# A hybrid decoder layer: the first branch's gates moved behind the attention and formed by products by sevens, the attention in single banks, sums in DRAM in 4 KB rows

## The chip, the cores and the metric

One core of one Trainium2 chip runs one decoder layer in float32. The metric is the device time of one launch in microseconds, median of three runs. Five queues of instructions work side by side on the core: PE (matmul, with its weight loads), DVE (VectorE), ACT (ScalarE), POOL (GpSimd) and SP (SyncE, here only DMA issues). Each works off its own instructions in order and waits at semaphores for the others.

## The reference

256 positions of 2048 channels go through three parallel token mixers and a feed-forward block. `h` is the normalised input, `p = h @ w_in` is cut into the mixers' inputs:

- A: `glu -> causal depthwise conv (31) -> LayerNorm -> silu -> @ w_a_out`
- B: `gelu(uv); u * (tril(W_s) LN(v) + b) -> @ w_b_out`
- C: attention with 16 query heads of 64 in 4 groups, and three sets of keys and values (compressed, selected, window) whose results are weighted by sigmoid gates per head, `-> @ w_c_out`

```python
g_a, g_b, g_c = jnp.split(jax.nn.sigmoid(merge_g), 3, axis=-1)
mixed = (g_a * y_a + g_b * y_b + g_c * y_c) @ w_o[l]
x = x + rms_norm(mixed, norm_mix_post[l])
...
u = causal_depthwise_conv(h @ w_up[l], ffn_conv_w[l], ffn_conv_b[l])
x = x + rms_norm((jax.nn.silu(u_g) * u_v) @ w_down[l], norm_ffn_post[l])
```

With 256 positions all four blocks of keys that a query may select are taken, so selected and window attention are both plain causal attention.

## The kernel before, in words

**Products.** A float32 weight piece of 128 x 1024 is loaded by SP into `wraw` (5 buffers), ACT copies it into a rounded part `whi`, DVE subtracts and leaves `wlo` (4 buffers each). A product of an activation tile with 512 columns is three matmuls, hi x hi, hi x lo, lo x hi (`mm_t`, L246 to L249). The positions are two tiles of 128, called t = 0, 1.

**Products by sevens.** Two tiles of the contraction (a pair), two halves of positions and two halves of columns are eight products of 128 x 128 by 512. Class `Seven` (L1034) forms them from seven products, Strassen's way in Winograd's form. The sums of activations are made on the core (`sums4`, L942, in `sh`), the sums of weights by POOL in DRAM before they are needed (`ahead_steps`, L132): a step copies a block of a weight into an `ahead` tile or adds one to it. The steps are one list, issued a few at a time by `ahead_by` (L155): a tiny `tick` copy waits for a mark of progress, then so many steps follow. `pooled` keeps them in order. A step that adds waits for the landing of the step whose result it adds to. `in_sevens` (L1114) interleaves plain tiles with sevens; `combine` adds up the four side banks, the totals (L1257) add them to the main banks.

**PSUM.** Eight banks of 128 x 512 float32: four of the pool `PS` (tag `acc`) and four of a second pool, which during the attention is cut into two single banks and one double (`banks(2, 1)`).

**Stages on PE, in the trace's time.** v of branch B (to 50 us), input of A, then u of B, keys, values and queries (to 296), then `branch(0)`: four times gates and outputs of B; `branch(1)`: the same of A (to 619), then gates and outputs of C (619 to 748), `w_o` (to 836), the feed-forward's up products (to 1328), down products (to the end). The gates of A and B are plain products of 16 tiles each, those of C take sevens for 4 of 8 pairs.

**Beside the products.** Convolution, norms and the attention are generators in a queue `bg`, of which `pump` takes steps between pieces of the main stream. The attention (`attn`, L961) has eight units, of a tile of positions, a half of the groups, and a branch. A unit's scores `s` are matmuls on 64 of the 128 rows, alternately lower and upper half (`in_turns`); its probabilities are transposed (`pp`), and the value products `O` fill 64 of 128 columns, again in pairs of halves. The compressed part enters `O` as one product with the tile `vbd`, which POOL fills (L969) from `pct`.

**The order.** The kernel's framework sets the order on each queue from dependencies, priorities and a timeline that it reckons; `issue_after` and `in_line` bind single instructions to others.

Of the kernel before, what the change touches and what calls it, by code (L numbers as in the profile page):

```python
# [30 lines left out]
D = 2048  # L31
# [17 lines left out]
BA, BB, BC, BG = 2100, 2200, 2200, 6500  # L49
# [15 lines left out]
def block(ctx: ExitStack, tc: tile.TileContext, x, xf, x0, fp, cst, rows, sgw, w1, w2, wf_a, wt_bv, wf_bu, wf_c,  # L65
# [66 lines left out]
    def ahead_steps():  # L132

        quads = [(("g", cp, j), wt_gq[cp, j], 3) for cp in range(2) for j in range(len(GP))]
# [4 lines left out]
        for i, (key, src, sums) in enumerate(quads):  # L139
# [180 lines left out]
    begin = P1.tile([128, T + KT], F32, name="begin")  # L320
# [16 lines left out]
    wz = P1.tile([128, 128], mybir.dt.bfloat16, tag="q", bufs=12, name="wz")  # L337
# [222 lines left out]
    def lna_gen():  # L560
# [61 lines left out]
    bg.append(mark("A"))  # L622
# [75 lines left out]
    def cmp_gen(kv):  # L698
# [22 lines left out]
        th = P1.tile([128, 2, 64], F32, tag="hth", name=f"hth{kv}")  # L721
# [132 lines left out]
    class Unit:  # L854
# [8 lines left out]
        def scores(self):  # L863
# [4 lines left out]
            ep = [Ct_box["ep"][:, r] if br else s8([128, 2, 4, 256], F32, f"ep{self.nm}{r}") for r in range(2)]  # L868
            e = self.e = [t[:, 0] for t in ep]
            self.pt = [t[:, 1].rearrange("p a b -> p (a b)").rearrange("p (k c) -> p k c", k=2) for t in ep]  # L870
            m = self.m = P1.tile([128, 2, 8], F32, tag="am", bufs=2, name="am" + self.nm)
            for b in range(4 // hpb):
                ps = two_banks([128, 2, hpb, nk], f"s{self.nm}{b}")
                in_turns([(ps[:, r, jj], qf[half[r], gg * 4 + b * hpb + jj, qt * 128:qt * 128 + 128],
                           kk[half[r], gg, br, 0:nk], True, True) for jj in range(hpb) for r in (1, 0)])
                for jj in range(hpb):
                    j = b * hpb + jj
                    for r in range(2):
                        V.tensor_tensor_reduce(e[r][:, j, 0:nk], ps[:, r, jj], mk, 1.0, -3e38, ALU.add, ALU.max,
                                               m[:, r, j:j + 1])  # L880
                        yield nk * 1.05 + 130
# [19 lines left out]
        def values(self, O):  # L901
            qt, gg, br = self.at
            e, pt = self.e, self.pt
            for kb in range(qt + 1):
                pp = two_banks([128, 2, 4, 128], f"pp{self.nm}{kb}")
                for r in range(2):
                    for j in range(4):
                        PE.transpose(pp[:, r, j], e[r][:, j, kb * 128:kb * 128 + 128], ident)
                for r in range(2):
                    with ExitStack() as order:  # L910
                        if r:
                            order.enter_context(tc.issue_after(a))
                        a = S.activation(pt[r][:, kb], pp[:, r].rearrange("p j t -> p (j t)"), AF.Copy).ins
                yield 200
            if br == 0:
                PE.matmul(O.rearrange("p j t -> p (j t)"), lhsT=vbd[:, gg], rhs=spread.rearrange("p j t -> p (j t)"),
                          start=True, stop=False, skip_group_check=True)
            in_turns([(O[half[r]].rearrange("p j t -> p (j t)"),
                       vsw[:, kb, br * 256 + (2 * gg + r) * 64:br * 256 + (2 * gg + r) * 64 + 64], pt[r][:, kb],
# [4 lines left out]
            Ct = Ct_box["t"]  # L924
# [6 lines left out]
    sh = P1.tile([128, 3, 2, 4, 128], R, name="sh")  # L931
    sh2 = []

    def sh_of(j):

        if j >= 3 and not sh2:
            sh2.append(s8([128, 2, 2, 4, 128], R, "sh2"))
        return sh[:, j] if j < 3 else sh2[0][:, j - 3]
# [3 lines left out]
    def sums4(a0, a1, dst, nm):  # L942
# [6 lines left out]
        for i, x in enumerate((p, q)):  # L949
            d = [dst[:, j, 2 * i:2 * i + 2].rearrange("p a b -> p (a b)") for j in range(2)]  # L950
# [3 lines left out]
    def input_sums(j):  # L954
# [3 lines left out]
        sums4(a[0], a[1], sh_of(j), f"h{j}")  # L958
        yield 0

    def attn():  # L961

        units = [Unit(qt, gg, br) for qt in range(2) for gg in range(2) for br in range(2)]
        yield from units[0].scores()
        for n, u in enumerate(units):
            if n + 1 < len(units):
                yield from units[n + 1].scores()
# [4 lines left out]
            if n % 2 and n // 2 < 3:  # L972
                yield from input_sums(n // 2)
# [4 lines left out]
    for qt in range(2):  # L978
        bg.append(apart(cmp_attn(qt)))

    def alloc_C():
        Ct_box["t"] = s16(P1, [128, 8, 2, T], R, "Ct")
        Ct_box["ep"] = s16(P1, [128, 2, 2, 4, T], F32, "ep")
        banks(2, 1)
        yield 0

    def single():
        banks(4, 0)
        yield 0
    bg.append(alloc_C())  # L990
# [43 lines left out]
    class Seven:  # L1034
# [25 lines left out]
        def seven(self, quad, key, a, tt, acts, nm, last):  # L1060
# [7 lines left out]
            if sums > 2:  # L1068
                nc.sync.dma_start(r[:, 512:], src[:, 2])
                parity[0] ^= 1  # L1070
                tt = tt[:, (L, U)[parity[0]]]
            if sums > 3:
                nc.sync.dma_start(tt, src[:, 3])
            (hb, lb), (ha, la), (ht, lt), (hr, lr) = (ring(nm + x) for x in "batr")
            high(hb, b)
            if sums > 2:
                rest(lb, b, hb)
                high(ha, a)
                if sums == 3:
                    fixed(V, V.tensor_add, tt, b[:, U], r[:, U])  # L1080
# [18 lines left out]
            for bank_, act, h, l, c in ((self.c[0][1], s4, hb, lb, L), (self.c[0][0], h1, hb, lb, U),  # L1099
# [14 lines left out]
    def in_sevens(pr, plain, pairs, REST, between, act, acts, keys, spare, tt, nm):  # L1114
# [3 lines left out]
        rest_ = REST[2:]  # L1118
# [806 lines left out]
```

## Time and profile before

| | |
|---|---|
| median of 3 runs | 1556.17 us (1554.79 to 1556.34) |
| span of the profiled execution, first to last instruction | 1554.3 us |
| median less this span | 1.9 us |
| PE matmuls | 8125 records |
| PE, DVE, ACT, POOL busy | 1547.5, 1289.7, 953.6, 214.2 us |
| queue of SP's loads (q1), of POOL's steps (q0) | 325.27 MB, 81.93 MB |

The page gives no other time of the profiled execution than its span. Busy times of PE overlap from one matmul to the next, so a busy share of 100% says that PE had no gap, and the distance between two starts says what a matmul costs. A row of the timeline is start, duration, engine, line, operation, output <- inputs, shape, count. A matmul that takes two passes over plain float32 (`s`, `O`) leaves two records. In the windows view each row is a stretch, its length, and the busy time of PE, PEld, DVE, ACT and POOL with the number of instructions, then PE's granted clock, the DMA share and GB/s.

### The profile page before, as it was taken

How to read it: one execution, taken by the hardware profiler on the slowest of the kernel's cores; microseconds unless marked ns; L12 is line 12 of the kernel's file. 1: busy time of each engine (PE TensorE's matmuls, PEld its weight loads, DVE VectorE, ACT ScalarE, POOL GpSimd, SP SyncE). 2: the span in 40 equal slices, each digit the busy share in tenths (PEclk: the TensorE clock that was granted, in tenths of full speed). 3: DMA queues.
4: the chain of work that ended last, by engine and by line, in shares of the span. 5: the costliest groups of instructions: out<-in, count | busy, mean ns of one | idle time of the engine just before them, and what ended most of it. 6: DMA issues, size and time to landing. Idle time of an engine off the chain costs nothing.

```text
span 1554.3 us, 23223 instructions
## 1 busy us (share of the span) xinstructions
PE 1547.5 (100%) x8125; PEld 1318.1 (85%) x8125; DVE 1289.7 (83%) x2189; ACT 953.6 (61%) x1518; POOL 214.2 (14%) x319
## 2 busy tenths in 40 slices
PE   9999999999999999999999999999999999999998
PEld 8888889888877777888888888888888888888887
DVE  7899999878675554878887888888888888899898
ACT  7644554467486756556565665656565656677774
POOL 1011350200111111000000022221212121100000
PEclk9999999999999999999999999999999999999999
DMA  9697996977777898767784699999999999989995
GB/s 369 197 269 234 274 295 211 286 255 242 212 223 234 218 258 259 237 221 253 269 263 157 208 294 307 303 281 262 270 271 264 266 256 268 317 279 348 318 374 210
DMA packets 130069, 409.33 MB, mean 263 GB/s; under 512 B 14240, under 2 KB 16016, under 8 KB 129184
## 3 DMA queue, kind: packets, MB, share of 16 engines
q1 hardware_dynamic: 97344, 325.27, 61.0%
q0 software_dynamic: 32032, 81.93, 23.3%
q8 instruction: 63, 1.03, 0.3%
q10 hardware_dynamic: 576, 0.66, 0.1%
q14 instruction: 54, 0.44, 0.1%
HBM read 399.67 MB, written 77.86 MB: 307 GB/s over the span
## 4 chain that ended last, share of the span: by engine, by line
PE 97%; DVE 1%; ACT 1%; issue 0%; DMA 0%; DVEq 0%; ACTq 0%
PE ps L226 29%; PE ps L233 15%; PE pd1a L1049 4%; PE pd0b L1049 4%; PE pg L248 3%; PE pg L249 3%; PE pg L247 3%; PE pd0a L1049 3%; PE pd1b L1049 3%; PE py L249 3%; PE py L247 3%; PE py L248 3%; PE pg0a L1049 2%; PE poa L1049 2%; PE pg1a L1049 2%; PE po L248 1%
## 5 line engine op out<-in xcount | busy, mean ns | idle before, releaser
L198 DVE TENSOR_TENSOR wlo<-wraw,whi 128x1024 fp32r<-128x1024 f32 (+1 forms) x376 | 455.4, 1216 | 122.8 <-ACT whi L197 103.2
L197 ACT ACTIVATE whi<-wraw 128x1024 fp32r<-128x1024 f32 (+1 forms) x376 | 394.7, 1055 | 241.6 <-PE ps L226 120.2
L226 PE MATMUL ps<-h2T,whi 128*128 128x512 f32 x1360 | 317.2, 390 | 0.0
L226 PEld LDWEIGHTS ps<-h2T,whi 128*128 128x128 f32 x1360 | 252.5, 188 | 50.3
L233 PEld LDWEIGHTS ps<-h2T,wlo 128*128 128x128 f32 x1360 | 169.4, 192 | 3.6
L233 PE MATMUL ps<-h2T,wlo 128*128 128x256 f32 x1360 | 170.8, 283 | 0.0
L226 PE MATMUL ps<-hT,whi 128*128 128x512 f32 x640 | 152.0, 391 | 0.0
L226 PEld LDWEIGHTS ps<-hT,whi 128*128 128x128 f32 x640 | 118.0, 188 | 22.9
L554 DVE SCALAR_TENSOR_TENSOR cv<-hb,fps,cv 128x256 f32<-128x256 f32 x240 | 103.8, 470 | 0.1
L248 PE MATMUL pg<-wlo,hT 128*128 128x512 f32 x256 | 101.2, 395 | 0.2 <-DVE wlo L198 0.2
L249 PE MATMUL pg<-whi,hT 128*128 128x512 f32 x256 | 101.1, 395 | 0.0
L247 PE MATMUL pg<-whi,hT 128*128 128x512 f32 x256 | 98.9, 394 | 0.3 <-ACT mg L1162 0.3
L1005 DVE TENSOR_TENSOR wlowraw<-wraw,whiwraw 128x1024 fp32r<-128x1024 f32 x58 | 70.4, 1222 | 32.0 <-ACT whiwraw L1005 30.6
L1536 ACT ACTIVATE fa<-fs,fps 128x256 f32<-128x256 f32 x88 | 52.7, 598 | 53.5 <-DVE fs L272 51.5
L233 PEld LDWEIGHTS ps<-hT,wlo 128*128 128x128 f32 x640 | 81.2, 192 | 2.5
L127 POOL DMA_DIRECT2D ahead<-in_wt_dq_dram x91 | 72.1, 906 | 80.1 <-DMA ahead<-in_wt_dq_dram 71.7
L233 PE MATMUL ps<-hT,wlo 128*128 128x256 f32 x640 | 82.8, 284 | 0.0
L1005 ACT ACTIVATE whiwraw<-wraw 128x1024 fp32r<-128x1024 f32 x58 | 61.0, 1058 | 32.4 <-PE py L249 12.7
L269 ACT ACTIVATE t<-ps 128x256 f32<-128x256 f32 x125 | 47.5, 381 | 51.2 <-PE ps L233 28.2
L127 POOL COPY tick<-gh 128x1 f32<-128x1 f32 x44 | 35.2, 800 | 271.6 <-ACT gh L1544 264.0
L248 PEld LDWEIGHTS pg<-wlo,hT 128*128 128x128 f32 x256 | 48.1, 188 | 11.7 <-issue 1.5
L247 PEld LDWEIGHTS pg<-whi,hT 128*128 128x128 f32 x256 | 47.9, 188 | 11.0 <-issue 0.9
(2173 smaller groups left out, 3085.2 us busy)
## 6 DMA issues: line engine op xcount, KB each, us to landing
wraw<-in_wf_up_dram SPq DMA_DIRECT2D x176, 512.0 KB, 6.1
ahead<-in_wt_dq_dram POOLq DMA_DIRECT2D x74, 512.0 KB, 9.3
wraw<-in_wt_g_dram SPq DMA_DIRECT2D x64, 512.0 KB, 5.0
wraw<-in_wt_p_dram SPq DMA_DIRECT2D x48, 512.0 KB, 5.7
wraw<-in_wt_dq_dram SPq DMA_DIRECT2D x33, 512.0 KB, 5.5
wraw<-in_wf_a_dram SPq DMA_DIRECT2D x32, 512.0 KB, 4.9
fin<-ahead SPq DMA_DIRECT2D x32, 512.0 KB, 5.7
ahead<-ahead POOLq DMA_DIRECT2D x45, 256.0 KB, 7.1
```

What stands on the lines that cost most here:

```text
L127: in_pool[:] = [op(*args, **kw).ins]
L197: S.activation(hi[:, :n], raw[:, :n], AF.Copy)
L198: V.tensor_sub(lo[:, :n], raw[:, :n], hi[:, :n].bitcast(F32))
L226: ins = PE.matmul(ps, lhsT=ws[k // 8][0][:, c:c + 128], rhs=mov[:, k], start=bool(k == 0 and first), stop=bool(k == n - 1 and not first), ...
L233: ins = PE.matmul(ps[:, 1], lhsT=ws[k // 8][1][:, c:c + 128], rhs=mov[:, k, 0], start=bool(k == 0 and not first), stop=bool(k == n - 1 and ...
L247: PE.matmul(ps, lhsT=xh, rhs=hi, start=first, stop=False)
L248: PE.matmul(ps, lhsT=xh, rhs=lo, start=False, stop=False)
L249: return PE.matmul(ps, lhsT=xl, rhs=hi, start=False, stop=last).ins
L554: V.scalar_tensor_tensor(ca[:, j], hb[:, j, k:k + T], w(j, k), ca[:, j], op0=ALU.mult, op1=ALU.add)
L1005: seq[eng] = [op(*args, **kw).ins]
L1049: ins = PE.matmul(bank, lhsT=a[x], rhs=w[y], start=first and j == 0, stop=bool(last and j == 2), skip_group_check=more).ins
L1536: S.activation(a, s, AF.Identity, bias=fps[:, C_FB + f:C_FB + f + 1], scale=w[2])
```

## The change

- **Order of the branches.** `branch` forms gates and outputs of B only. Then `outs_a` forms A's outputs alone, ungated, into `ya` (DVE copies). The gates of A become columns of the gate products behind it.
- **Gates.** `gates_7` runs four times by sevens, twice for A (i = 0, 1), twice for C (i = 2, 3), for 4 of 8 pairs each. Main and side banks swap between the two pools from one to the next. A's gates are applied by `gate_a`: multiply `ya`, add to `mac`. With `lead` some plain tiles go first, and `then` puts the previous group's totals and `gate_a` behind them.
- **Attention.** It starts with the last part of A's norm (`lnz_gen`), the scores of the first unit and the compressed scores taken in turn, and works off the units of the second tile of positions first. It has to be finished in the first group of gates (`attended`). Scores and transposes take single banks, one per half, from a pool of four throughout. `pump` is scaled by 0.85 from the attention on.
- **Sums.** The weights' four blocks are laid out in another order in DRAM, so that a step that adds two blocks reads them as one row of 4 KB, where it read two rows of 2 KB. There are 32 steps more (eight more pairs), and `ahead_by` takes (4, 8, 8, 8) of them in `branch` and (8, 8, 8, 8) in `outs_a`, where the two branches took (0, 0, 6, 8) and (8, 8, 8, 0).

Three places show how instructions move. On PE, scores and value products of a unit of the second tile of positions; `py`, `pg` are full products, `whi`, `wlo` weights, the number behind a name is its buffer. Before:

```order
L850 MATMUL O_4589<-ep_4435,kkv 64x512
L850 MATMUL O_4589<-ep_4434,kkv 64x512
L850 MATMUL s_4607<-kkv,qf 128x256 x4
L249 MATMUL py_5354<-whi_5394,At 128x512
...
L247 MATMUL pg_5446<-whi_5449,hT 128x512
L850 MATMUL s_4616<-kkv,qf 128x256 x4
L248 MATMUL pg_5446<-wlo_5450,hT 128x512
```

And in the change, of such a unit too:

```order
L853 MATMUL O_4415<-pt_3282,kkv 64x512 x2
L853 MATMUL s_4633<-kkv,qf 128x256
L249 MATMUL py_5234<-whi_5244,At 128x512
L250 MATMUL py_5234<-wlo_5245,At 128x512
L251 MATMUL py_5234<-whi_5244,At 128x512
L249 MATMUL py_5235<-whi_5244,At 128x512
L853 MATMUL s_4632<-kkv,qf 128x256
L853 MATMUL s_4633<-kkv,qf 128x256
L853 MATMUL s_4632<-kkv,qf 128x256
L250 MATMUL py_5235<-wlo_5245,At 128x512
L853 MATMUL O_4415<-ep_4334,kkv 64x512 x2
L853 MATMUL s_4643<-kkv,qf 128x256
```

A group of four scores stood in one piece; now the first of the four stands alone, and its partner on the other half of the array comes four products later, from another bank. On POOL, the fill of `vbd` for the last compressed unit. Before:

```order
L127 DMA ahead_82<-ahead_82 128x512 [waits DMASW2_49,DMASW1_49]
L127 DMA ahead_83<-in_wt_dq_dram 256x512 [waits DMASW3_49]
L969 TENSOR_TENSOR vbd<-pct_4313,cs 128x512 [waits PE_49]
L127 COPY tick<-mac 128x1 [waits DVE_49,Pool_49]
L127 DMA ahead_84<-in_wt_dq_dram 128x1024 [waits DMASW6_49]
```

In the change, with the second and third of the `ya` batches ahead of it:

```order
L129 DMA ahead_90<-in_wt_dq_dram 128x1024 [waits DMASW0_49]
L129 DMA ahead_91<-in_wt_dq_dram 128x1024
L129 COPY tick<-ya 128x1 [waits DVE_49,Pool_49]
L129 DMA ahead_90<-ahead_90 128x512 [waits DMASW2_49,DMASW1_49]
L129 DMA ahead_91<-in_wt_dq_dram 128x1024 [waits DMASW3_49]
L129 DMA ahead_92<-in_wt_dq_dram 128x1024 [waits DMASW6_49]
L129 DMA ahead_92<-in_wt_dq_dram 128x512 [waits DMASW7_49]
L990 TENSOR_TENSOR vbd<-pct_4529,cs 128x512 [waits PE_49]
```

It stood behind the second of the batches that follow `mac` and now stands in the middle of the third that follows `ya`, with DMA steps on both sides. The diff, cut:

```diff
 def pump(ns):
+    if "attn" in marks:
+        ns *= RUSH
...
-        quads = [(("g", cp, j), wt_gq[cp, j], 3) for cp in range(2) for j in range(len(GP))]
+        quads = [(("g", cp, j), wt_gq[cp, j], 3) for cp in range(4) for j in range(len(GP))]
...
             if sums > 2:
-                yield dst[:, 2:], src[:, 0:sums - 2], {}
+                yield dst[:, 2:], src[:, 4 - sums:2], {}
             yield from late
-            yield dst[:, 0:2], src[:, 0:4:2], add
-            late = [(dst[:, b], dst[:, b - 1], add) for b in range(2, sums)]
+            yield dst[:, 0:2], src[:, 1:3], add
+            late = [(dst[:, x], dst[:, y], add) for x, y in ((sums - 1, 1), (2, 3))[:sums - 2]]
...
-                ps = two_banks([128, 2, hpb, nk], f"s{self.nm}{b}")
-                in_turns([(ps[:, r, jj], qf[half[r], gg * 4 + b * hpb + jj, qt * 128:qt * 128 + 128],
+                ps = [bank([128, hpb, nk], f"s{self.nm}{b}{r}") for r in range(2)]
+                in_turns([(ps[r][:, jj], qf[half[r], gg * 4 + b * hpb + jj, qt * 128:qt * 128 + 128],
...
-            for kb in range(qt + 1):
-                pp = two_banks([128, 2, 4, 128], f"pp{self.nm}{kb}")
+            for kb in range(qt, -1, -1):
+                pp = [bank([128, 4, 128], f"pp{self.nm}{kb}{r}") for r in range(2)]
...
-        units = [Unit(qt, gg, br) for qt in range(2) for gg in range(2) for br in range(2)]
-        yield from units[0].scores()
+        units = [Unit(qt, gg, br) for qt in (1, 0) for gg in range(2) for br in range(2)]
+        yield from in_turn(lnz_gen(), apart(cmp_attn(1)), apart(units[0].scores()))
+        marks.add("A")
...
-            ahead_by(mac[:, 0, cb * 512:cb * 512 + 1], ((0, 0, 6, 8), (8, 8, 8, 0))[bi][cb])
+            ahead_by(mac[:, 0, cb * 512:cb * 512 + 1], (4, 8, 8, 8)[cb])
             pump(BUDGET)
+
+    def outs_a():
+        for cb in range(4):
+            py = [PS.tile([128, 512], F32, tag="acc", name=f"py1{cb}{t}") for t in range(2)]
+            for q in range(2):
+                hs = granule(wt_p[(4 + cb) * 2 + q])
+                if cb == 0 and q == 0:
+                    until("A")
...
+                        pe_last[0] = mm_t(py[t], At[:, k, 0, ts], At[:, k, 1, ts], hi[:, c], lo[:, c], k == 0, k == 7)
...
+                    V.tensor_copy(ya[:, t, cb * 512:cb * 512 + 512], py[t])
+            ahead_by(ya[:, 0, cb * 512:cb * 512 + 1], (8, 8, 8, 8)[cb])
...
-    branch(0, lambda: Bt_box["t"])
-    branch(1, lambda: At)
-    until("A")
-    until("C")
+    branch()
+    ya = s16(P1, [128, 2, D], F32, "ya")
+    outs_a()
...
+    def gate_a(cp, gates):
         for n in range(2):
             for t in range(2):
+                cc = slice(cp * 1024 + n * 512, cp * 1024 + n * 512 + 512)
+                V.scalar_tensor_tensor(gates[:, t, n], gates[:, t, n], 1.0, ya[:, t, cc], op0=ALU.add, op1=ALU.mult)
+                V.tensor_add(mac[:, t, cc], mac[:, t, cc], gates[:, t, n])
...
+    prs.append(gates_7(0, (0, 0, 0, 0), 6, attended))
+    prs.append(gates_7(1, (1, 0, 0, 0), 4, gated_a(0)))
+    for cp in range(2):
+        pr = gates_7(2 + cp, (1, 1, 1, 0) if cp else (1, 0, 0, 0), 2 if cp else 4, None if cp else gated_a(1))
```

More of the change, by code (lines that the diff above doesn't have):

```diff
@@ L589, in lna_gen, with lnz_gen @@
         r = rsqrt(P1, var, T, "a")
+        norm["r"] = r
         yield 3400
-        while "gates" not in marks:
-            yield 2400
+    def lnz_gen():
+        r = norm["r"]
         for j in range(8):
@@ L621, in block @@
     bg.append(lna_gen())
-    bg.append(mark("A"))
     BUDGET = BB
@@ L929, in values @@
             yield 650
[L931 to L938, printed above, removed]
+    pt1 = P1.tile([128, 2, 4, 128], F32, name="pt1")
+    sh = P1.tile([128, 4, 2, 3, 128], R, name="sh")
     H1, H2 = slice(0, 128), slice(128, T)
@@ L948, in sums4 @@
         V.tensor_sub(q[:, H2], a0[:, H1], a0[:, H2])
-        for i, x in enumerate((p, q)):
-            d = [dst[:, j, 2 * i:2 * i + 2].rearrange("p a b -> p (a b)") for j in range(2)]
+        first, last = dst
+        for d, x in (([first[:, j, 0:2].rearrange("p a b -> p (a b)") for j in range(2)], p),
+                     ([first[:, j, 2] for j in range(2)], q[:, H1]), (last, q[:, H2])):
             S.activation(d[0], x, AF.Copy)
@@ L957, in input_sums, with g_acts, in_turn @@
             V.tensor_add(a[i], hT[:, 2 * j + i, 0].bitcast(F32), hT[:, 2 * j + i, 1].bitcast(F32))
[L958 to L959 removed]
+        s3.append(P1.tile([128, 2, 128], R, tag="q", bufs=11, name=f"s3{j}"))
+        sums4(a[0], a[1], (sh[:, j], [s3[j][:, i] for i in range(2)]), f"h{j}")
+        yield 3000
+    s3 = []
+    def g_acts(j):
+        return acts_of(j, GP[j], hx, (s3[j][:, 0], s3[j][:, 1]))
+    def in_turn(*works):
+        works = list(works)
+        while works:
+            for w in list(works):
+                try:
+                    yield next(w)
+                except StopIteration:
+                    works.remove(w)
     def attn():
[L963 to L964 removed]
+        units = [Unit(qt, gg, br) for qt in (1, 0) for gg in range(2) for br in range(2)]
+        yield from in_turn(lnz_gen(), apart(cmp_attn(1)), apart(units[0].scores()))
+        marks.add("A")
+        Ct_box["t"] = s16(P1, [128, 8, 2, T], R, "Ct")
         for n, u in enumerate(units):
             if n + 1 < len(units):
[L967 removed]
+                if n == 1:
+                    yield from in_turn(apart(cmp_attn(0)), units[n + 1].scores())
+                else:
+                    yield from units[n + 1].scores()
             if u.at[2] == 0:
@@ L971, in attn @@
             yield from u.weights()
-            if n % 2 and n // 2 < 3:
-                yield from input_sums(n // 2)
+            if SUMS_AT <= n < SUMS_AT + 4:
+                yield from input_sums(n - SUMS_AT)
             if u.at[2] == 0:
@@ L976, in attn @@
             yield from u.values(O)
[L978 to L990, printed above, removed]
+    bg.append(mark("attn"))
     bg.append(attn())
-    for j in range(3, len(GP)):
-        bg.append(input_sums(j))
-    bg.append(single())
     bg.append(mark("C"))
@@ L1112, in total, with in_sevens @@
             return V.tensor_sub if n else V.tensor_add
-    def in_sevens(pr, plain, pairs, REST, between, act, acts, keys, spare, tt, nm):
+    def in_sevens(pr, plain, pairs, REST, between, act, acts, keys, spare, tt, nm, lead=2, then=None):
         todo = [(k, weights(plain[REST.index(k)])) for k in REST[0:2]]
         pr.k_tiles(todo, act, t_first=True)
-        rest_ = REST[2:]
+        for k in REST[2:lead]:
+            pr.k_tiles([(k, weights(plain[REST.index(k)]))], act)
+        if then:
+            then()
+        rest_ = REST[lead:]
         for j in range(len(between)):
@@ L1122, in in_sevens @@
                 pr.k_tiles([(k, weights(plain[REST.index(k)]))], act)
-            pr.seven(pairs[j], (*keys, j), spare(j), tt, acts(j), f"{nm}{j}", j == len(between) - 1)
+            pr.seven(pairs[j], (*keys, j), spare(j), tt(), acts(j), f"{nm}{j}", j == len(between) - 1)
         for k in rest_:
@@ L1233, in hx, with acts_of @@
         return hT[:, k, 0, ts], hT[:, k, 1, ts]
-    def acts_of(j, pair, x):
-        s1, s2, s4, s3 = parts(sh_of(j), range(4))
-        return s4, x(2 * pair + 1, H1), s3, s1, s2, x(2 * pair + 1, H2), x(2 * pair, H1)
+    def acts_of(j, pair, x, last):
+        s1, s2, s4 = parts(sh[:, j], range(3))
+        return (s4, x(2 * pair + 1, H1), last, s1, s2, x(2 * pair + 1, H2), x(2 * pair, H1))
     def wp(cb, k):
@@ new lines, in four, with gates_7, begin @@
+    def four(i, side):
+        if bool(i == 1) != bool(side):
+            return [bank([128, 512], f"pg{i}{side}{x}") for x in range(4)]
+        return [PS.tile([128, 512], F32, tag="acc", name=f"pg{i}{side}{x}") for x in range(4)]
+    gates_of, box = [], {}
+    def gates_7(i, between, lead=2, then=None):
+        pr = Seven(four(i, ""), [None] * 4)
+        pr.at = lambda t, n: gates_of[i][:, t, n]
+        def begin():
+            if then:
+                then()
+            pr.p1, pr.p5, pr.p6, pr.p7 = four(i, "s")
+            gates_of.append(s8([128, 2, 2, 512], F32, f"gates{i}"))
+        in_sevens(pr, wt_gp[i], wt_gq[i], GREST, between, hx, g_acts, ("g", i), lambda j: box["qa"][:, j % 2],
+                  lambda: box["tt"], f"g{i}", lead, begin)
+        return pr
@@ new lines, in attended, with gated_a, then @@
+    def attended():
+        until("C")
+        pump(1e6)
+        box["tt"] = P1.tile([128, 1024], F32, tag="vbd", name="tt")
+        box["qa"] = s8([128, 2, 1024], F32, "qa")
+    def gated_a(cp):
+        def then():
+            totals(prs[cp])
+            gate_a(cp, gates_of[cp])
+        return then
+    prs = []
+    prs.append(gates_7(0, (0, 0, 0, 0), 6, attended))
+    prs.append(gates_7(1, (1, 0, 0, 0), 4, gated_a(0)))
+    for cp in range(2):
+        pr = gates_7(2 + cp, (1, 1, 1, 0) if cp else (1, 0, 0, 0), 2 if cp else 4, None if cp else gated_a(1))
+        gates = gates_of[2 + cp]
+        if cp == 0:
+            mh, ml = mix["h"], mix["l"] = [s16(P1, [128, KT, T], R, "m" + x) for x in "hl"]
+            Ct = Ct_box["t"]
+        early = [wp(2 * cp, k) for k in (0, 2)]
+        totals(pr, (0,))
+        early.append(wp(2 * cp, 4))
+        totals(pr, (1,))
```

127 lines of the change are left out of this document (64 added, 63 removed).

## The prediction

> **What bounds the kernel now.** First the page's busy shares and its chain of waits, then PE's own list of waits, then two stages in the windows view.
>
> ```profile
> span 1554.3 us, 23223 instructions
> PE 1547.5 (100%) x8125; PEld 1318.1 (85%) x8125; DVE 1289.7 (83%) x2189; ACT 953.6 (61%) x1518; POOL 214.2 (14%) x319
> PE 97%; DVE 1%; ACT 1%; issue 0%; DMA 0%; DVEq 0%; ACTq 0%
> PE warm L341 <- DVE wz L338: 1.1, 1, 1.1
> PE pg L247 <- ACT mg L1162: 0.3, 1, 0.3
> PE pg L248 <- DVE wlo L198: 0.2, 1, 0.2
> ...
> 401.00:625.00 224.00, 223.73 (x1103) 173.68 (x1102) 134.26 (x322) 142.22 (x320) 35.48 (x48) 1.00 0.82 232
> 1385.00:1440.00 55.00, 55.00 (x243) 45.48 (x243) 53.29 (x60) 38.76 (x45) 2.15 (x4) 1.00 0.95 330
> ```
>
> PE is busy in the whole span, 97% of the chain that ended last is PE, and the three waits listed are all it has: 1.6 us. The granted clock is 1.00. So the time is the length of PE's instruction stream, and the change is worth what it does to that stream, plus whatever waits it brings in. The attention stage (401 to 625 us) runs without a wait with DVE busy 60% and ACT 63%; the last product stage without one with DVE busy 53.29 of 55 us and DMA at 0.95. A full DVE does not by itself stop PE.
>
> **What the change removes from PE: 24 products, 5.4 us.** Counted in the two orders, PE has 8005 matmuls before and 7981 after. All 24 are 512 columns wide: 2 groups of gate columns, 4 pairs each, one of eight products of three matmuls saved per pair. Busy times overlap, so the price is the cadence of starts.
>
> ```profile
> 562.37 0.39 PE L248 MATMUL pg<-wlo,hT 128*128 128x512 f32 x1
> ...
> 564.18 0.39 PE L247 MATMUL py<-whi,At 128*128 128x512 f32 x1
> ```
>
> The rows left out hold seven more matmuls: eight starts in 1.81 us, 0.2266 us each. 24 x 0.2266 = **5.4 us less**.
>
> **What it adds to PE: more, and more broken, half-array blocks.** The scores `s` (64 rows) and the value products `O` (64 columns) use half of the array at a time; two halves run as a pair. The order of before has them in 14 blocks between full products, each group of scores whole. In the order of the change I count 23 blocks, because single banks come free one by one: "one s, some products, three s". What a block costs:
>
> ```profile
> 584.55 0.39 PE L247 MATMUL pg<-whi,hT 128*128 128x512 f32 x1
> 584.87 1.14 PE L850 MATMUL s<-kkv,qf 64*128 64x256 f32 x8
> ...
> 586.51 0.39 PE L247 MATMUL pg<-whi,hT 128*128 128x512 f32 x1
> ...
> 584.87 0.92 PE L850 MATMUL s<-kkv,qf 64*128 64x256 f32 x6
> 584.87 0.70 PE L850 MATMUL s<-kkv,qf 64*128 64x256 f32 x4
> ...
> 575.50 0.39 PE L249 MATMUL py<-whi,At 128*128 128x512 f32 x1
> 575.82 1.94 PE L850 MATMUL O<-ep,kkv 128*64 128x512 f32 x8
> 577.69 1.13 PE L850 MATMUL s<-kkv,qf 64*128 64x256 f32 x8
> 578.75 0.50 PE L247 MATMUL py<-whi,At 128*128 128x512 f32 x1
> 579.09 0.39 PE L248 MATMUL py<-wlo,At 128*128 128x512 f32 x1
> 579.32 0.40 PE L249 MATMUL py<-whi,At 128*128 128x512 f32 x1
> ```
>
> Each matmul of two passes leaves two records, so x8 is a group of four. Two further records, one of each half, lengthen the block by 0.21 us (the same block cut at x4, x6 and x8: 0.70, 0.92, 1.14). From 584.55 to 586.51, the third product start behind the block, are 1.96 us; three full products take 0.68 of it, the group's body 4 x 0.21 = 0.84, and 0.44 us is what entering and leaving cost. The block at 575.82 holds two O pairs (0.84 each) and the same s body: from 575.50 to 579.32, 3.82 - 0.68 - 2.52 = 0.62, so a join inside a block costs 0.2 instead of another 0.44. Nine more blocks: 9 x 0.44 = 4.0; joins, 8 against 6 before: 0.4. Together **4.4 us more**.
>
> A broken pair is not in the trace. A lone half costs between half a pair (0.11 per record, nothing lost) and a whole one. The nearest row is the full-array product of the same type and width as O:
>
> ```profile
> 518.33 0.40 PE L248 MATMUL pg<-wlo,hT 128*128 128x512 f32 x1
> 518.57 1.02 PE L916 MATMUL O<-vbd 128*128 128x512 f32 x2
> ...
> 520.13 0.39 PE L249 MATMUL pg<-whi,hT 128*128 128x512 f32 x1
> ```
>
> Four full products stand in these 1.80 us, so one such matmul costs 0.89 us, and a pair of O halves 0.84. A matmul alone takes the time of a pair; I take that for a lone half too. Broken are five groups of 256 columns (0.42 us each) and three of 128 (0.21): **2.7 us more**, or 0 at the low end. (By the Trainium skill, "TensorEngine Tiling (Array Packing)", Theoretical Speedup, two tiles side by side give up to 2x, so a half left alone would take as long as the pair; no run here shows one.)
>
> Sum on PE: -5.4 + 4.4 + 2.7 = **+1.7 us**. Low end -5.4 with neither blocks nor pairs costing, -1.0 with free pairs.
>
> **What lies beside.** The weight pieces of the gates (ACT, then DVE) stay ahead of PE. In a run of products by sevens:
>
> ```profile
> 646.62 1.23 DVE L1005 TENSOR_TENSOR wlog03b<-wraw,whig03b 128x1024 fp32r<-128x1024 f32 x1 [1.09 <-ACT whig03b L1005]
> 647.76 0.68 DVE L1005 TENSOR_TENSOR tt<-wraw,wraw 128x512 f32<-128x512 f32 x1
> 648.37 1.22 DVE L1005 TENSOR_TENSOR wlog03a<-qa,whig03a 128x1024 fp32r<-128x1024 f32 x1
> ...
> 651.42 2.58 DVE L1005 TENSOR_TENSOR wlowraw<-wraw,whiwraw 128x1024 fp32r<-128x1024 f32 x2
> ```
>
> One seven takes DVE 651.42 - 646.62 = 4.80 us (1.14 per wide piece, 0.61 per narrow operation) and PE 21 x 0.2266 = 4.76. From the first seven of the first gate group to the end of the third group PE has 468 products, 106 us; DVE has 12 sevens (57.6), 18 plain pieces (20.5), three combines of four (7.3), two totals of four (4.9) and 16 operations for gate times `ya` and the sum in `mac` (9.8): 100 us. It fits, 94% full, under a load like that of 1385 to 1440. If that cover fails, see the third rival.
>
> The attention is squeezed: from the first scores to the last O there are 503 full products in the order instead of some 783, so about 114 + 53 us instead of 224.
>
> ```profile
> L198 DVE TENSOR_TENSOR wlo<-wraw,whi 128x1024 fp32r<-128x1024 f32 x61 | 74.2, 1223 | 57.1 <-ACT whi L197 56.5
> L197 ACT ACTIVATE whi<-wraw 128x1024 fp32r<-128x1024 f32 x60 | 63.0, 1059 | 52.0 <-PE pg L249 36.8 <-PE py L249 14.2 <-ACT pct L837 1.0
> ```
>
> Some 20 fewer weight pieces fall into it: ACT 142 - 21 = 121 us of 167, DVE 134 - 24 = 110, each with under 15 us of moved work from the first branch's norm. No engine is full, so I cost it at nothing. Ten more steps of the DRAM sums are left for the feed-forward stage (96 instead of 86, by the table in `ahead_by`); they lie beside PE there, where a DMA share of 1.02 cost no wait:
>
> ```profile
> 920.00:980.00 60.00, 60.00 (x355) 53.47 (x354) 51.59 (x92) 37.12 (x60) 14.61 (x22) 1.00 1.02 318
> ```
>
> **The rivals.** First, **POOL comes late**, the slower case. POOL's queue carries the sums in DRAM, and each step that adds waits for a landing. `vbd<-pct` (L969), which PE's `O<-vbd` needs, is queued behind them, and everything on PE behind `O<-vbd`.
>
> ```profile
> 536.91 0.18 POOL L127 COPY tick<-mac 128x1 f32<-128x1 f32 x1 [21.27 <-DVE mac L1195]
> ...
> 561.02 1.61 POOL L127 DMA_DIRECT2D ahead<-in_wt_dq_dram  x2 [10.17 <-DMA ahead<-in_wt_dq_dram]
> 577.15 0.25 POOL L127 COPY tick<-mac 128x1 f32<-128x1 f32 x1 [14.52 <-DVE mac L1195]
> ...
> 600.03 0.89 POOL L127 DMA_DIRECT2D ahead<-in_wt_dq_dram  x1 [2.21 <-DMA ahead<-in_wt_dq_dram]
> L969 POOL TENSOR_TENSOR vbd<-pct,cs x4: 1034/1112/1802, 414.6 to 479.3; 128x512 f32<-128x512 f32 x4
> ahead<-in_wt_dq_dram POOLq DMA_DIRECT2D x74, 512.0 KB, 9.3
> ahead<-ahead POOLq DMA_DIRECT2D x45, 256.0 KB, 7.1
> ```
>
> Eight steps take 25.7 us (to 562.6) and 23.8 us; the batches start 40 us apart. After, batches follow every 12 to 18 us. Between the last `mac` tick and the fourth `vbd<-pct` stand 28 steps: at 24.8 us for eight 87 us, with two `vbd` 89. PE reaches the fourth `O<-vbd` after 207 full products (46.9), 12 blocks with 8 joins (6.9), their bodies (13.2), two vbd (1.8) and 60 transposes (6.6): 75 us. PE would stand 14 us. But by the new order only seven landings lie one behind the other on that chain; at 8.2 us, the middle of 9.3 and 7.1, they take 57 us, and some 25 issues at 0.6 us between them 15: 72 us, just in time, and 4 KB rows may shorten them further. Point of decision: 75/28 = 2.7 us per step. I price it half way, 6 us: 1557.9 + 6 = **1564**. What speaks for larger rows:
>
> ```profile
> q1 hardware_dynamic: 97344, 325.27, 61.0%
> q0 software_dynamic: 32032, 81.93, 23.3%
> ```
>
> Of 16 engines x 1554.3 us, q0 holds 0.181 us per packet of 2.56 KB and q1 0.156 per 3.34 KB: bytes are cheaper in larger packets. (The Trainium skill, "DMA: Bandwidth & Descriptors", Specifications, puts full rate at 512 B and above, so by it 2 KB rows lose nothing and 4 KB win nothing; then a step keeps its time and this rival holds.)
>
> Second, **blocks cost less than counted**: the products' 5.4 us arrive nearly whole, 1556.2 - 5 = **1551**. Against it: 0.44 us is in the rows of every isolated block.
>
> Third, **DVE is late in the gates**: with totals and gate times `ya`, DVE has 4 x 1.14 + 12 x 0.61 = 11.9 us beside four plain pieces of PE (10.9), then sevens at 4.80 against 4.76. Twice 1.2 us, if nothing was ahead: 1557.9 + 2.4 = **1560**.
>
> **The numbers.** The sum is against the profiled span, 1554.3; the median of the runs shown, 1556.17, lies 1.9 above it, and I keep that distance. Forecast: no change that can be told, 1556.2 + 1.7 = **1557.9**, chance 0.50. POOL late 0.26, DVE late 0.12, blocks cheap 0.12. Under 0.2% (3.1 us) a change can't be told here; the forecast's own range is 1555 to 1559, and of the third rival's chance nearly all counts as slower: faster 0.12, same 0.50, slower 0.38. The range, 1552 to 1565, takes in POOL late and most of the low ends of the unknown costs.
>
> **What would show it.** Right: PE's list of waits stays under 3 us; the excess of s and O blocks over full products grows by about 7 us between 390 and 560 us; the gates stage starts near 530 us and PE has 24 fewer 512-wide matmuls. POOL late: PE idle before `O<-vbd`, released by POOL `vbd`. DVE late: PE idle at `pg` rows, released by `wlog` pieces or gates. Wrong altogether: a lone s record that takes 0.1 us, or 64-row blocks without a gap on either side.

## The result: 1579.5 us, 1.5% slower, and the profile after

| | before | after |
|---|---|---|
| median of four runs | 1555.84 us (1554.79 to 1556.34) | 1579.47 us (1574.79 to 1581.26) |
| span of the profiled execution | 1554.3 us | 1573.1 us |
| PE waits in that execution | 1.6 us | 13.1 us |

The profiled execution of the change is the shortest of its four, 1574.79 us; what the other three took beyond it is in no profile. The ratio is 1.0146, with a 95% interval of 1.013 to 1.0162. The forecast was 1557.9, no change that can be told. The page of the changed kernel, its busy shares and its chain of waits:

```profile
span 1573.1 us, 23354 instructions
PE 1555.0 (99%) x8101; PEld 1317.6 (84%) x8101; DVE 1320.8 (84%) x2229; ACT 969.3 (62%) x1536; POOL 219.7 (14%) x351
PE 90%; DMA 6%; DVE 2%; issue 1%; ACT 1%; POOL 1%; SPq 0%; DVEq 0%; ACTq 0%; POOLq 0%
```

Before, PE alone was 97% of that chain and DMA 0%. Now DMA is 6% of it, 94 us. PE's list of waits in the changed kernel (engine, line, what is waited for; us in total, times, longest):

```profile
PE O L922 <- POOL vbd L990: 6.2, 1, 6.2
PE pg L1055 <- DVE wlowraw L1011: 3.3, 2, 2.5
PE pg L1055 <- ACT whiwraw L1011: 1.2, 1, 1.2
PE warm L343 <- DVE wz L340: 1.1, 1, 1.1
...
```

There are two stalls: one before the last `O<-vbd`, the other in the gates. Together with some smaller waits they are 11.5 us more than before, and the span is 18.8 us longer. The windows view of the changed kernel around the two stalls shows most of the rest in PE's granted clock, the third number from the end:

```profile
547.00:552.00 5.00, 4.99 (x11) 3.28 (x12) 0.51 (x1) 1.06 (x1) 0.00 (x0) 0.55 0.97 252
552.00:560.00 8.00, 8.00 (x38) 5.67 (x36) 3.77 (x4) 5.31 (x11) 1.37 (x2) 1.00 0.77 193
560.00:600.00 40.00, 39.24 (x173) 30.94 (x172) 27.32 (x29) 21.58 (x25) 7.43 (x11) 1.00 1.01 328
603.00:608.00 5.00, 1.29 (x4) 0.56 (x4) 5.00 (x8) 4.45 (x6) 0.00 (x0) 0.81 0.15 57
608.00:613.00 5.00, 5.00 (x13) 3.86 (x13) 4.81 (x6) 0.20 (x1) 0.00 (x0) 0.51 0.68 200
```

Behind each stall PE is busy for 5 us at little more than half its clock. In the 5 us from 608 on it starts 13 products, where 22 fit (5 / 0.2266), so a stall costs its own length and about 2 us on top. In the timeline of the changed kernel's PE:

```profile
547.01 2.07 PE L922 MATMUL O<-vbd 128*128 128x512 f32 x2 [6.21 <-POOL vbd L990]
...
550.59 0.63 PE L1055 MATMUL pg<-wlowraw,hT 128*128 128x512 f32 x1
551.01 0.84 PE L1055 MATMUL pg<-whiwraw,hT 128*128 128x512 f32 x2
...
607.65 0.80 PE L1055 MATMUL pg<-wlowraw,hT 128*128 128x512 f32 x1 [2.50 <-DVE wlowraw L1011]
```

From 550.59 to 551.01 are 0.42 us for one product, against 0.2266 elsewhere. (The Trainium skill, "TensorE: Matmul & The Clock Gate", Part 1: The HAM clock gate, has the array at half rate after an idle window of about 3.4 us, until a busy window has passed. The trace agrees with the half rate. It does not bear out 3.4 us of idleness as the condition: in one run below, a single wait of 2.4 us was enough.)

**First stall.** POOL's queue in the changed kernel, between the last tick on `mac` and the fourth fill of `vbd` (the third fill stands at 500.93):

```profile
465.39 0.18 POOL L129 COPY tick<-mac 128x1 f32<-128x1 f32 x1 [21.71 <-DVE mac L1202]
...
533.74 1.37 POOL L129 DMA_DIRECT2D ahead<-in_wt_dq_dram  x2 [8.24 <-DMA ahead<-in_wt_dq_dram]
...
541.76 0.85 POOL L129 DMA_DIRECT2D ahead<-ahead  x1 [6.46 <-DMA ahead<-in_wt_dq_dram]
543.98 1.92 POOL L129 DMA_DIRECT2D ahead<-in_wt_dq_dram  x3 [1.36 <-DMA ahead<-in_wt_dq_dram]
545.59 1.37 POOL L990 TENSOR_TENSOR vbd<-pct,cs 128x512 f32<-128x512 f32 x1
```

The fill ends 81.6 us behind the tick. PE stood ready at 540.8, 75.4 us behind it.

**Second stall.** ACT and DVE in the changed kernel, where PE waits until 607.65:

```profile
595.55 1.06 ACT L1011 ACTIVATE whiwraw<-wraw 128x1024 fp32r<-128x1024 f32 x1 [5.11 <-DMA wraw<-in_wt_gp_dram]
598.14 1.06 ACT L1011 ACTIVATE whiwraw<-wraw 128x1024 fp32r<-128x1024 f32 x1 [1.53 <-DMA wraw<-in_wt_gp_dram]
...
599.24 1.23 DVE L1011 TENSOR_TENSOR wlowraw<-wraw,whiwraw 128x1024 fp32r<-128x1024 f32 x1 [1.36 <-ACT whiwraw L1011]
600.38 2.48 DVE L1011 TENSOR_TENSOR gates<-pg,gates 128x512 f32<-128x512 f32 x4
...
606.38 1.22 DVE L1011 TENSOR_TENSOR wlowraw<-wraw,whiwraw 128x1024 fp32r<-128x1024 f32 x1
```

The releaser named is DVE: 6 us of totals and gate times `ya` stand between two weight pieces. But the piece ahead of them, at 599.24, was itself late: DVE waited for ACT, and ACT for loads, 5.11 us for the one before and 1.53 for this one. Two readings are open, and the experiments tell them apart.

### The profile page after: what moved, and what is told of

It reads as the page before. It is cut to its first block, busy times and chain, and to the rows that moved or that the text cites. A ratio compares the mean times of both kernels' runs of the same rounds, so it can differ in the third digit from the quotient of the medians.

```text
span 1573.1 us, 23354 instructions
## 1 busy us (share of the span) xinstructions
PE 1555.0 (99%) x8101; PEld 1317.6 (84%) x8101; DVE 1320.8 (84%) x2229; ACT 969.3 (62%) x1536; POOL 219.7 (14%) x351
## 4 chain that ended last, share of the span: by engine, by line
PE 90%; DMA 6%; DVE 2%; issue 1%; ACT 1%; POOL 1%; SPq 0%; DVEq 0%; ACTq 0%; POOLq 0%
PE ps L228 29%; PE ps L235 15%; PE pg L1055 7%; PE pd1a L1055 4%; PE pd0b L1055 4%; PE pd0a L1055 3%; PE pd1b L1055 3%; DMA ahead<-in_wt_dq_dram 2%; DMA ahead<-in_wt_oq_dram 2%; PE poa L1055 2%; PE py L250 2%; PE py L251 2%; PE py L249 2%; PE pg L250 1%; PE pg L251 1%; PE pg L249 1%
## 5 line engine op out<-in xcount | busy, mean ns | idle before, releaser
L200 DVE TENSOR_TENSOR wlo<-wraw,whi 128x1024 fp32r<-128x1024 f32 (+1 forms) x344 | 417.5, 1218 | 91.7 <-ACT whi L199 73.3
L199 ACT ACTIVATE whi<-wraw 128x1024 fp32r<-128x1024 f32 (+1 forms) x344 | 361.7, 1056 | 206.3 <-PE ps L228 117.2
L1011 DVE TENSOR_TENSOR wlowraw<-wraw,whiwraw 128x1024 fp32r<-128x1024 f32 x74 | 89.8, 1222 | 42.8 <-ACT whiwraw L1011 40.8
L1011 ACT ACTIVATE whiwraw<-wraw 128x1024 fp32r<-128x1024 f32 x74 | 78.0, 1059 | 55.2 <-PE pg L1055 13.2
L1055 PE MATMUL pg<-whiwraw,hT 128*128 128x512 f32 x256 | 85.3, 407 | 1.2 <-ACT whiwraw L1011 1.2
L129 POOL DMA_DIRECT2D ahead<-ahead x53 | 43.8, 827 | 206.9 <-DMA ahead<-in_wt_dq_dram 74.7
L1055 PEld LDWEIGHTS pg<-whiwraw,hT 128*128 128x128 f32 x256 | 49.6, 194 | 14.4 <-issue 2.1
L1614 DVE SCALAR_TENSOR_TENSOR fa<-fs,fps,fa 128x255 f32<-128x255 f32 x88 | 42.3, 481 | 16.6 <-ACT fa L1613 16.5
L1055 PE MATMUL pg<-wlowraw,hT 128*128 128x512 f32 x128 | 51.8, 404 | 3.3 <-DVE wlowraw L1011 3.3
```

What stands on the lines that cost most here:

```text
L129: in_pool[:] = [op(*args, **kw).ins]
L199: S.activation(hi[:, :n], raw[:, :n], AF.Copy)
L200: V.tensor_sub(lo[:, :n], raw[:, :n], hi[:, :n].bitcast(F32))
L1011: seq[eng] = [op(*args, **kw).ins]
L1055: ins = PE.matmul(bank, lhsT=a[x], rhs=w[y], start=first and j == 0, stop=bool(last and j == 2), skip_group_check=more).ins
```

## The experiments

**Theory 1:** both stalls come from the steps of the DRAM sums that are issued behind A's outputs; the first through POOL's queue, the second because the last of them share the DMA engines with the gates' weight loads. **Theory 2:** the second stall is DVE's own chain. All kernels below were timed beside the kernel before on the same chip.

### Take either away: the fill to another engine, or the steps to a later stage

First, all four fills go from POOL to DVE:

```diff
-                G.tensor_mul(spread, pct[u.at[0]][:, u.at[1]]...
+                V.tensor_mul(spread, pct[u.at[0]][:, u.at[1]]...
```

> The four fills of vbd go to DVE, nothing else moves. Theory 1 (POOL's queue of DMA steps made the fourth fill late, and a last batch of steps that shares the DMA engines with the gates' weight loads makes the second stall): the 6.2 us wait before the last O<-vbd is gone together with the slow matmuls right behind it (0.427 us a product instead of 0.227, about 2 us), but the stall near 603 us stays or grows to at most 10 us, since the gates now start 8 us sooner and the last batch of steps does not; span 1564 to 1568. Theory 2 (the second stall is DVE's own chain of totals and gate times ya ahead of the next weight piece): the second stall is as in the changed kernel, 5.2 us and 2.7 us of slow matmuls, span 1564. Rival: the fill is late for its input, not for its queue: the wait before O<-vbd stays 6 us, now released by DVE; span 1573.

Then, from the changed kernel again, the third and fourth batch behind A's outputs are left for the feed-forward stage:

```diff
-            ahead_by(ya[:, 0, cb * 512:cb * 512 + 1], (8, 8, 8, 8)[cb])
+            ahead_by(ya[:, 0, cb * 512:cb * 512 + 1], (8, 8, 0, 0)[cb])
```

> The third and fourth batch of DMA steps behind A's outputs (16 steps) are left for the feed-forward stage; the fill of vbd stays on POOL. Theory 1: no wait before O<-vbd, no late weight load in the gates (DMA share near 540 to 590 us under 0.9), so both stalls and the slow matmuls behind them go, 9 and 8 us: span 1555 to 1558. Theory 2: only the first stall goes, the second stays at 4 to 5 us of DVE waits with slow matmuls behind: span 1564. Rival (the feed-forward has no room for 16 more steps, with a DMA share of 1.0 there): PE waits at ps rows appear, and the end is later than by theory 1 by several us.

Measured: 1565.53 us with the fill on DVE (ratio 1.0054, interval 1.0039 to 1.0069; before 1556.57), 1558.05 us with the steps moved (ratio 1.0008, 0.9999 to 1.0018). With the fill on DVE, PE's list of waits has:

```profile
PE pg L1055 <- DVE wlowraw L1011: 2.5, 1, 2.5
...
PE pg L1055 <- ACT whiwraw L1011: 1.1, 1, 1.1
```

The first stall is gone, the second is there; the span, 1562.7 us, is a little below what theory 1 gave. With the steps moved, the longest wait is the 1.1 us at the kernel's start, although DVE does the same work in the gates. The windows view of that kernel there:

```profile
560.00:600.00 40.00, 40.00 (x177) 33.00 (x177) 38.22 (x45) 26.37 (x30) 0.00 (x0) 1.00 0.73 246
```

DVE is busy 38.22 of 40 us and PE does not wait once. The same 6 us of totals and gate times `ya` stand between two weight pieces there:

```profile
583.48 1.23 DVE L1011 TENSOR_TENSOR wlowraw<-wraw,whiwraw 128x1024 fp32r<-128x1024 f32 x1 [0.22 <-ACT whiwraw L1011]
584.62 2.48 DVE L1011 TENSOR_TENSOR gates<-pg,gates 128x512 f32<-128x512 f32 x4
...
590.63 1.22 DVE L1011 TENSOR_TENSOR wlowraw<-wraw,whiwraw 128x1024 fp32r<-128x1024 f32 x1
```

So DVE's chain alone makes no stall, which refutes theory 2. The loads show why. Landing times in the gates, of the changed kernel (560 to 600 us), with POOL's steps among them:

```profile
wraw<-in_wt_gp_dram SPq DMA_DIRECT2D x7, 512.0 KB, 8.9
ahead<-in_wt_dq_dram POOLq DMA_DIRECT2D x6, 512.0 KB, 9.1
```

And with the steps moved (555 to 595 us):

```profile
wraw<-in_wt_gp_dram SPq DMA_DIRECT2D x7, 512.0 KB, 5.0
```

The same load takes 5.0 us alone and 8.9 beside the steps, where the DMA share was 1.01 (560 to 600 us). Whether the DMA engines or the memory behind them set this is not shown. Where PE starts its stages shows what each stall cost (us, from the timelines of PE; a seven is a product by sevens):

| start of | change | fill on DVE | steps moved |
|---|---|---|---|
| first gate product of B | 296.61 | 296.85 | 296.50 |
| first seven of the first gate group | 565.25 | 556.64 | 556.32 |
| first seven of the second gate group | 612.51 | 601.98 | 595.78 |
| first product of `w_o` | 767.19 | 756.63 | 750.24 |

Up to the first seven the change takes 268.6 us, the other two 259.8: the late fill with its slow clock costs 8.8. From there to the first seven of the second group they take 47.3, 45.3 and 39.5: the steps beside the gates cost 7.8 us in the change and 5.9 with the fill on DVE. Why this stall is 1.9 us longer behind the first one is not shown. Of the 18.8 us there remain 0.8 in other places between the change and the kernel with the steps moved, and 1555.7 - 1554.3 = 1.4 us for everything else in the change.

### Half of it: only the last batch, and a single step

The fill on DVE and only the fourth batch left out, `(8, 8, 8, 0)`:

> The changed kernel with vbd filled by DVE and only the fourth batch of steps behind A's outputs (8 steps) left for later. If the second stall comes from the last batch sharing the DMA engines with the gates' weight loads between 565 and 592 us, it is gone: span 1556 to 1557. If the third batch, which runs to about 567 us, matters too, half of the stall's 7 us stays: 1559.

Measured: 1559.63 us (1557.55 to 1564.10; ratio 1.0027, 1.0016 to 1.0038). The spans of the six executions go from 1555.8 to 1562.4 us, with a median of 1557.9, between the two halves of the expectation. The profiled one is the longest. In it the third batch alone, which POOL works off from 545 to 578 us, still makes one wait in the gates, with half clock behind it:

```profile
PE pg L1055 <- DVE wlowraw L1011: 2.4, 1, 2.4
...
600.00:602.00 2.00, 2.00 (x6) 1.61 (x5) 2.00 (x3) 0.00 (x0) 0.00 (x0) 0.50 0.73 199
```

So the third batch can reach into the gates, but not in every execution: the shortest, at 1555.8 us, is as short as with both batches moved (1555.7) and leaves no room for this stall.

From the changed kernel, the third batch cut to one step, `(8, 8, 1, 0)`, the fill on POOL behind it:

> The changed kernel with the third batch cut to one step and the fourth left for later; vbd on POOL behind that step. The step adds to a block that lands near 542 us, so vbd is ready near 543.5 us and PE, there at 540.4, waits about 3 us. If a wait of this length already slows the products behind it as 6.2 us did, some 10 to 15 products take 0.427 us and the total is 5 to 6 us above the kernel without the third batch (span 1561); if not, 3 us (1559).

Measured: 1571.96 us (ratio 1.0103, 1.0084 to 1.0121), a miss. The wait is 9.7 us, not 3. POOL's queue in this kernel:

```profile
540.99 1.35 POOL L129 DMA_DIRECT2D ahead<-in_wt_dq_dram  x2 [11.41 <-DMA ahead<-in_wt_dq_dram]
...
550.58 0.84 POOL L129 DMA_DIRECT2D ahead<-ahead  x1 [8.04 <-DMA ahead<-in_wt_dq_dram]
551.14 1.35 POOL L990 TENSOR_TENSOR vbd<-pct,cs 128x512 f32<-128x512 f32 x1
```

And the same place of the queue with both batches moved:

```profile
533.95 1.35 POOL L129 DMA_DIRECT2D ahead<-in_wt_dq_dram  x2 [7.33 <-DMA ahead<-in_wt_dq_dram]
```

The wait that is 11.41 in the one was 7.33 in the other, though the queue ahead of it is the same; in the changed kernel it was 8.24. One landing on the way to a fill can thus cost 4 us more in one execution than in another, and one added step put the fill a whole landing later. A further 2.4 us of its span lie in the kernel's first products (see the last section). Whether a wait of 3 us slows the clock was not answered by this run; in the run above a wait of 2.4 us did.

### The row size alone

The changed kernel with two rows of 2 KB again, and the kernel before with rows of 4 KB (in both, the weights' blocks laid out to suit):

```diff
...
-            yield dst[:, 0:2], src[:, 1:3], add
+            yield dst[:, 0:2], src[:, 0:4:2], add
...
```

> The changed kernel with the DRAM sums read in two rows of 2 KB per partition again. If larger rows shorten a step (in the profile of before a q0 packet of 2 KB takes 0.211 us and one of 4 KB 0.183), each adding step of 512 KB takes 2 to 4 us longer, so by theory 1 the fourth fill of vbd comes 5 to 15 us later and the last batch runs deeper into the gates: span 1580 to 1595. If row size does not matter: the same waits, span 1573 to 1579 like the changed kernel.

> The kernel before with only the 4 KB rows. PE does not wait for the sums there, so the time is that of before within 1.5 us (1554 to 1557) either way; if larger rows shorten a step, batches of eight on POOL end 3 to 6 us sooner than the 24 to 26 us of before, and if they do not, they take as long.

Measured: 1576.32 us (1569.35 to 1580.31) with 2 KB rows, against 1579.47 for the change: the same within the scatter of both. The kernel before with 4 KB rows: 1556.90 us (ratio 1.0001, 0.9992 to 1.0011). With 2 KB rows the wait for the fill was 4.9 us longer, and the waits in the gates were shorter, 2.9 us instead of 4.5, perhaps because PE came to them later:

```profile
PE O L922 <- POOL vbd L990: 11.1, 1, 11.1
PE pg L1055 <- DVE wlowraw L1011: 2.5, 1, 2.5
...
```

The chain from the tick to the fill took 86 us here and 82 in the changed kernel. That is one execution of each, and one landing alone scattered by 4 us above, so it is not shown that the rows shorten it. In the kernel before, two batches of eight steps took 24.4 and 22.4 us with 4 KB rows and 25.7 and 23.8 without: 1.3 us less each, not the 3 to 6 that were expected if rows matter. There q0's share of the engines fell from 23.3% to 22.6%:

```profile
q0 software_dynamic: 26272, 81.93, 22.6%
```

That is 3% for 18% fewer packets. The single packets in the trace show why. Before, no adding step had packets of 4 KB on q0; there were 8800, of 0.183 us on average. With the adding steps among them there are 14560, of 0.266 us, so that one of an adding step takes about 0.39 (an estimate from these two averages). It replaces two of 2 KB, of 0.211 us each. The estimate from packets took the price of a copy for that of an addition. (By the Trainium skill, "DMA: Bandwidth & Descriptors", Specifications, a transfer needs no more than 512 B for full rate; the 3% are nearer to that than to the estimate from packets that the prediction drew on.)

### The price of blocks and broken pairs

The kernel with 16 steps moved, and the attention's rate changed, which moves the half-array blocks among the products:

```diff
-BA, BB, BC, BG, RUSH, SUMS_AT = 2100, 2200, 2200, 6500, 0.85, 4
+BA, BB, BC, BG, RUSH, SUMS_AT = 2100, 2200, 2200, 6500, 0.70, 4
```

> The kernel of the run before with 16 steps left for later (span 1555.7), with the attention's steps taken from the queue at 0.70 instead of 0.85 of the rate. By its order PE has 20 half-array blocks instead of 23 and 5 broken pairs instead of 8. If blocks and broken pairs are priced as in the prediction (0.44 us a block, 0.42 or 0.21 us a pair), it is 2.4 us faster: span 1553.3, just ahead of the kernel before. If only full products count, it is the same: 1555.7. If slowing the attention makes it late for the gates, a PE wait appears before the last O products and it is slower.

> The same with the attention's rate at 1.10: 20 blocks, 9 joins, 6 broken pairs in the order. By the prices of the prediction 2.0 us faster, span 1553.7; the fill of vbd is needed earlier, so if its distance (ready some 4 us ahead at 0.85) is used up, PE waits for POOL again, a few us with slow products behind them.

Measured at 0.70: 1556.35 us (ratio 1.0004, 0.9995 to 1.0013), the best version found and level with the kernel before. First gate product and first product of `w_o`, at 0.85 and then, in the second fence, at 0.70:

```profile
296.50 0.63 PE L249 MATMUL pg<-whi,hT 128*128 128x512 f32 x2
...
750.24 0.39 PE L1055 MATMUL poa<-whiwraw,mh 128*128 128x512 f32 x1
```

```profile
298.94 0.63 PE L249 MATMUL pg<-whi,hT 128*128 128x512 f32 x2
...
561.44 0.50 PE L1055 MATMUL pg0s<-whig00r,hT 128*128 128x512 f32 x1 [0.38 <-DVE Ct L932]
...
750.80 0.39 PE L1055 MATMUL poa<-whiwraw,mh 128*128 128x512 f32 x1
```

453.74 against 451.86 us: 1.9 less, with one new wait of some 0.5 us in it, so 2.4 for three blocks and three broken pairs, as priced, in one execution of each. The 2.4 us by which the stretch begins later at 0.70 lie in the first products of the kernel, which neither change touches.

Measured at 1.10: 1559.06 us (ratio 1.0022, 1.0012 to 1.0031). A miss, and not through `vbd`: in the profiled execution, the longest of ten, PE reaches the attention's pieces before the other engines have them.

```profile
PE O L853 <- ACT ep L919: 1.5, 1, 1.5
PE s L853 <- DVE am L881: 0.7, 1, 0.7
```

### Four more steps away

At 0.70, the first batch behind B's outputs goes too, `(0, 8, 8, 8)` for `(4, 8, 8, 8)`, and the same at 0.75:

> The kernel with 16 steps left for later and the attention's rate at 0.70, and the first batch of four steps, behind the first columns of B's outputs, left for later too (20 steps moved in all). If the waits of PE near 370 us (1.1 us in the list of waits, some 1.4 us with what they break) come from weight loads that share the DMA engines with that batch (DMA share 0.93 at 340 to 360 us, 0.59 in the kernel before), they go, and the stretch from the first gate product to the first product of w_o falls from 451.9 to 450.5 us, where the kernel before has 451.9: 1.4 us, about 0.1%, faster than before. If DVE's own small operations ahead of the weight piece make them, nothing changes: as before within 0.1%.

> The same with the attention's rate at 0.75: by its order 19 blocks, 11 joins, 6 broken pairs, by the prices of the prediction 0.6 us slower than at 0.70; if the wait for the last Ct (0.4 us at 0.70) goes with it, the same time.

Measured: 1559.28 us (ratio 1.0020, 1.0011 to 1.0029) and 1560.99 us (1.0029, 1.0021 to 1.0038), both slower than expected. From the first gate product to the first product of `w_o` the profiled executions take 451.8 and 452.6 us, the first as in the second half of its expectation, the second 0.8 slower, near the 0.6 priced; what is lost lies behind. The waits near 370 us stay at 0.6 and 0.5 us though the DMA share at 340 to 360 us fell from 0.93 in the changed kernel to 0.74 here. So the loads do not make them; that DVE's small operations do is the reading left, and was not tried. And 20 steps are too many for the feed-forward stage, where 16 were free. The first of the two kernels waits in the down products, for pieces of weight sums (the second too, 2.3 us); that these waits are the whole loss is not shown:

```profile
PE pd0a L1055 <- DVE wloq_8a L1011: 0.8, 1, 0.8
PE pd0b L1055 <- DVE wloq_11b L1011: 0.7, 1, 0.7
```

## Why the prediction was wrong, point by point

- **The sum on PE, +1.7 us: right.** With both stalls taken away by moving 16 steps, the same PE stream takes 1.4 us more by the spans and 1.5 by the medians (the interval of the ratio, 0.9999 to 1.0018, takes in no change too). Blocks and pairs were tested together, by the attention's rate: 2.4 us, as priced.
- **The broken pair, open in the prediction: a lone half costs what a pair costs.** In the kernel with the steps moved, a group of four is cut into one and three:

```profile
413.27 0.40 PE L251 MATMUL py<-whi,Bt 128*128 128x512 f32 x1
413.60 0.70 PE L853 MATMUL s<-kkv,qf 64*128 64x256 f32 x2
414.22 0.50 PE L249 MATMUL py<-whi,Bt 128*128 128x512 f32 x1
414.56 0.40 PE L250 MATMUL py<-wlo,Bt 128*128 128x512 f32 x1
414.79 0.40 PE L251 MATMUL py<-whi,Bt 128*128 128x512 f32 x1
415.12 1.13 PE L853 MATMUL s<-kkv,qf 64*128 64x256 f32 x6
```

  From 413.27 to 414.79 are three products (0.68) and a block of 0.84; less 0.44 for entering and leaving, 0.40 for the lone half, where a pair is 0.42. The three that are left (x6) take 1.13 us, where a whole group of four (x8) took 1.14.
- **DVE in the gates, 94% full and at nothing: right with loads in time.** 38.22 of 40 us without a wait. The list of waits named DVE in the changed kernel, and yet the DVE rival was not the cause; the loads ahead of it were late.
- **The attention, squeezed and at nothing: right**, but with little to spare. A rate of 1.10 already makes PE wait for ACT and DVE there.
- **The steps of the DRAM sums, at nothing: the step that failed.** The prediction costed the ten more that are left for the feed-forward stage, and these were free, as were 16 further ones. It did not follow the 32 that were put behind A's outputs to where they run. The last batches of them fall into the gates of the products by sevens, which had no steps before. "The weight pieces of the gates (ACT, then DVE) stay ahead of PE" was reckoned from DVE's work alone, under the load of another stage, a DMA share of 0.95. With the steps the share was 1.01, the weight loads took 8.9 us instead of 5.0, and the pieces came late. That is 7.8 us in the changed kernel and 5.9 with the fill on DVE, in no term and in no rival.
- **POOL late: the right mechanism, with too small a chance.** The range for the fill, 72 to 89 us behind the tick, held the 81.6 measured, PE came to it after 75.4 us, where 75 were counted, and the wait was 6.2 where 6 was priced. That agreement is partly luck: 6 was a middle between two counts, and neither was right. The count that spoke for "just in time" had seven landings (57 us) and issues (15). In the trace the seven long waits are 52.9 us; issues, ticks and the third fill take 22, and short waits between them 6.5. The issues were the term that was mis-sized. The price had no slow clock in it: the fill's lateness cost 8.8 us up to the first seven, nearly half of the 18.8, and without it the span is 10.4 us shorter.
- **That 4 KB rows might shorten the steps:** not to an extent that matters. Eight steps took 1.3 us less in the kernel before, and the 5 us over the whole chain here are within the scatter of landings.

## What to carry to other kernels

Follow every moved transfer to the stage in which it will run, and set it against the loads of that stage: an engine's work by its count of instructions can fit while its loads no longer do. A compute instruction in a queue of dependent DMA steps inherits all their landings, so give it another engine, or keep the steps behind it. And where a wait is attributed to a busy engine, look one releaser further back before the engine is blamed.

## What the runs showed of the hardware that was not expected

- **A stall of PE costs more than its length.** Behind waits of 2.4, 6.2, 9.7 and 11.1 us, and behind 3.6 us in two pieces, products ran at half clock for about 3 to 5 us, and the stretch around each was 1.7 to 2.6 us longer than its wait. A wait of 0.8 us at 597 in the changed kernel left the clock at full. In the kernel without the fourth batch, though, products ran at half clock from 369.9 to 372.9 behind waits of 0.2, 0.5 and 0.8 us, so from which length a wait has this price is not settled. How long the slow part lasts did not follow the length of the wait: 5 us behind 3.7, less than 3 behind 11.1.
- **The first products of the kernel run at half rate in some executions.** In three profiles (rate 0.70, rate 1.10, a single step) they took 0.42 us each until 9 to 10 us, where the others have 0.23 from about 6 us on, and the rest came 2 us later. The windows view gives their granted clock as 1.00, so that this is the clock is not shown. The wait ahead of them does not decide it: 0.5 to 0.9 us in these three, and 0.5, 0.8, 0.9 and 1.6 us in four others that ran at the full rate. The runs at rate 0.70 lie in two groups, six at 1555.2 to 1556.4 and five at 1557.8 to 1558.2; that the groups have this cause is argued from one profile.
- **Landings scatter.** POOL's long waits for a landing, in the chain ahead of the fill, take 5.5 to 11.4 us, and the same one differs by 4 us from one execution to another. A chain of them can be late by a landing in one execution and not in the next, as the 6.5 us between the changed kernel's shortest and longest run may show; only the shortest was profiled.
